# The first two pairs of each MLP with eight block products, and the feature sums made between them

## The chip, the cores and the metric

One core of a Trainium2 chip runs the whole program. The metric is the device time in microseconds, from the start of the program to its end; the median of three runs is compared. TensorE (PE in the rows) multiplies, VectorE (DVE), ScalarE (ACT) and GpSimd (POOL) do the element-wise work, and SyncE (SP) issues the transfers.

## The reference, cut to what matters

Two layers of a backbone over 1280 tokens (1024 latent tokens and a context of 256) with 1024 features; each layer is a mixer and then an MLP with 4096 hidden features and squared ReLU.

```python
def modulate(x, g, shift, scale):
    return (rms_norm(x, g) * (1.0 + scale) + shift).astype(x.dtype)

def sq_relu_mlp(h, w1, w2):
    return jnp.square(jax.nn.relu(h @ w1)) @ w2
...
        yp = yp + (mp[5] * sq_relu_mlp(modulate(yp, norm2_g[l], mp[3], mp[4]), ff_w1[l], ff_w2[l])).astype(yp.dtype)
        ys = ys + (ms[5] * sq_relu_mlp(modulate(ys, norm2_g[l], ms[3], ms[4]), ff_w1[l], ff_w2[l])).astype(ys.dtype)
```

Everything is float32. The kernel splits each operand into a high part (type fp32r) and the low part that is left (`hi`, `lo`), and makes a product of two float32 blocks from three matmuls (hi by hi, hi by lo, lo by hi): this is `three`.

## The kernel before

Activations lie with features on partitions: `hhi[ti]`, `hlo[ti]` are the normalised input of the MLP, [128, 8 feature chunks, tokens], for the token parts ti = 0 (tokens 0 to 511), 1 (512 to 1023) and 2 (the 256 context tokens). They are made by `apply` of a norm object for each token part, which takes the rows of 1/rms that TensorE spreads over the partitions (`rows`: two matmuls, `spread_rows`, L368 and L369, from a diagonal matrix `ndg` that VectorE and ScalarE make, L361 and L362; its input `nrs` comes from a power on GpSimd, L403, and `nst` from VectorE, L401).

`ff1` makes the hidden features in 16 pairs of chunks (128 features each). For the 1024 latent tokens a pair is a 2 by 2 block product: two chunks by two halves of the input features (feature chunks 0 to 3 and 4 to 7) times these halves by two halves of the tokens. Plainly that is eight block products of 12 matmuls (4 feature chunks, `three` for each). The kernel takes seven, as Winograd's variant of Strassen's scheme does: sums of weight blocks (`sum_` on GpSimd, L601, split again by `parts`, L607 and L608, into `s12` and `s34`) times sums of feature blocks (`com[2]`, `com[3]`, `com[4]`, the tiles tb2, tb3 and tb4h/tb4l). The feature sums are made once for an MLP, inside `apply` of token part 1 (tb2 and tb3, through the tiles nd) and of token part 2 (`last_block`: tb4h, tb4l from nd4). The context tokens add 2 times 24 matmuls 256 wide to each pair (`prompt`).

The raw weights of a pair are loaded into four `wraw` slots or, for odd pairs, into one tile with the tag `tt`, which holds nd4 before, and the first feature blocks of `ff2` after. At the end of a pair four differences of hidden blocks are made (L668) and all is written to device memory (`Dt`, `Dh`); `ff2` reads it back (`br`), with its weights in `ar`.

The instructions of each engine stand in one order, which a list scheduler makes at build time; an engine does not go past an instruction that waits. SyncE issues every transfer from one queue. `pend` in `ff1` holds the statistics and the `apply` of token part 2, which are emitted between the first products of pair 0 (`late`).

Of the kernel before, what the change touches and what calls it, by code (L numbers as in the profile page):

```python
# [431 lines left out]
class NormBlocks(Norm):  # L432
# [17 lines left out]
    def apply(self, At, Bt, hhi, hlo):  # L450
        if self.ti == 2:
            Norm.apply(self, At, Bt, hhi, hlo)
            self.last_block()
# [11 lines left out]
        d2, d3 = [[g.fp.tile([128, 2, 512], F32, tag="hid", name="nd", bufs=4) for i in range(2)] for _ in range(2)]
        com["d4"] = g.fp.tile([128, 4, 512], F32, tag="tt", name="nd4", bufs=1)
        x0 = com["x0"]
        for k in range(4):
            u, v = self.scaled(k, pb, At), self.scaled(4 + k, pb, At)
            t, e2, e3 = x0[:, k, :], d2[k // 2][:, k % 2], d3[k // 2][:, k % 2]  # L470
            nc.vector.tensor_tensor(t, u, t, op=ALU.subtract)
            nc.vector.tensor_tensor(e2, v, t, op=ALU.subtract)
            nc.gpsimd.tensor_tensor(e3, v, u, op=ALU.subtract)
            nc.gpsimd.tensor_tensor(com["d4"][:, k], x0[:, 4 + k, :], e2, op=ALU.subtract)
            self.plain(hi[:, k, :], lo[:, k, :], t)
            self.biased(hi[:, 4 + k, :], lo[:, 4 + k, :], v, Bt[:, 4 + k, 0:1])
        for n, (d, tag) in enumerate(((d2, "x0"), (d3, "x1"))):
            t = g.xm.tile([128, 2, 4, 512], F32R, tag=tag, name=f"tb{2 + n}", bufs=1)
            for k in range(4):
                self.biased(t[:, 0, k], t[:, 1, k], d[k // 2][:, k % 2], Bt[:, 4 + k, 0:1] if n == 0 else dsh[:, k:k + 1])  # L480
            com[2 + n] = (t[:, 0], t[:, 1])

    def last_block(self):
        g, com = self.g, self.com
# [81 lines left out]

def ff1(g, l, h, com, pend, Dh, Dt):
# [42 lines left out]

    for p in range(NFC // 2):
# [10 lines left out]
        sum_(a22, a21, a22, ALU.add)  # L622
        sum_(a21, a11, a21)
        sum_(a11, a22, a11)
        sum_(a12, a12, a11)
        s12, s34 = parts((a22, a11), nc.vector), parts((a21, a12), nc.gpsimd)
# [14 lines left out]
        ca = bank(g, "mm")
        product(ca, w1, 0, part(0, 0), True)
        late()
        t = saved(ca)
        ps = bank(g, "w")
        product(ps, w1, 1, part(0, 4), True)
        late()
        add_square(b11, t, ps)
        if p:
# [1 line left out]
        product(ca, s12, 1, com[2], False)
        u1 = saved(ca)
        cb = bank(g, "w")
        product(cb, s12, 0, part(1, 0), True)
        product(ca, s34, 0, com[3], False)
        u2 = saved(ca)
# [3 lines left out]
        prompt(1, w2)  # L660
        product(ca, w2, 1, com[4], False)
        square(b21, ca)
        product(cb, s34, 1, part(1, 4), False)
        add_square(b12, u1, cb)
        ts = []
        for j, (x, y) in enumerate(((b12, b11), (b22, 0), (b22, b12), (b21, 1))):
            ts.append(scratch())
            nc.vector.tensor_tensor(ts[j], x, ts[y] if j % 2 else y, op=ALU.subtract)  # L668
            nc.sync.dma_start(Dt[p, :, j], ts[j])
# [1499 lines left out]
```

## Time and profile before

| | us |
|---|---|
| median of 3 runs | 3257.35 (3252.08 to 3261.74) |
| the profiled execution, its own time | 3254.04 |
| its span, first to last instruction | 3251.1 |
| TensorE busy in the span | 3009.4 (93%) |
| VectorE / ScalarE / GpSimd busy | 2171.6 / 1292.5 / 1286.6 |
| mean granted TensorE clock | 0.965 of full speed |

The two MLPs' first halves (`ff1`) run from about 1067 us to 1530 us and from about 2384 us to 2845 us of the span. A row of a timeline gives the start, the duration, the engine, the line and what is written from what; in brackets stands how long the engine sat idle before it and what it waited for.

### The profile page before, as it was taken

The page shows a single profiled execution, that of the slowest core. Times are in us where ns is not written, and L with a number is a line of the kernel's source. Part 1 is how long each engine was busy: PE and PEld are TensorE (multiplying, and loading weights), DVE is VectorE, ACT ScalarE, POOL GpSimd, SP SyncE. Part 2 cuts the span into 40 slices and gives each one's busy share as a digit, 9 for nine tenths or more (in the row PEclk, how much of TensorE's full clock was granted, in tenths as well). Part 3 has the DMA queues.
Part 4 walks back from the last instruction along what each step waited for, and adds up shares of the span by engine and source line. Part 5 has one row for each costly group of instructions (what it writes and reads, how often), then busy time and mean ns, then how long its engine had stood idle before and what let it go on. Part 6 is the DMA issues. An engine that isn't in the chain of part 4 may idle for free.

```text
span 3251.1 us, 50543 instructions
## 1 busy us (share of the span) xinstructions
PE 3009.4 (93%) x19543; PEld 2411.1 (74%) x19543; DVE 2171.6 (67%) x3278; ACT 1292.5 (40%) x2116; POOL 1286.6 (40%) x861
## 2 busy tenths in 40 slices
PE   8989976899999699999999998998969999999999
PEld 5777754665557588887888877887757888788888
DVE  5548887667742855556877766878276555687776
ACT  5455433453322422222333336778242222333332
POOL 0000004455421645445767631000155444667664
PEclk9999986999999899999999999999989999999999
DMA  5356677546862233336624220110413333464332
GB/s 203 85 142 175 174 181 195 155 125 208 264 226 72 71 111 133 132 133 213 231 92 156 91 98 27 40 39 23 153 38 123 139 127 127 168 238 156 123 111 85
DMA packets 309967, 437.52 MB, mean 135 GB/s; under 512 B 80346, under 2 KB 154874, under 8 KB 309726
## 3 DMA queue, kind: packets, MB, share of 16 engines
q1 hardware_dynamic: 309726, 434.29, 41.8%
q8 instruction: 153, 2.51, 0.3%
q14 instruction: 88, 0.72, 0.1%
HBM read 301.29 MB, written 132.90 MB: 134 GB/s over the span
## 4 chain that ended last, share of the span: by engine, by line
PE 62%; DVE 16%; issue 7%; DMA 4%; ACT 2%; POOL 2%; SPq 1%; DVEq 0%; ACTq 0%; POOLq 0%
PE ps_w L556 7%; PE ps_w L557 7%; PE ps_w L558 7%; PE ps_mm L558 6%; PE ps_mm L556 6%; PE ps_mm L557 6%; PE ps_mm L528 4%; PE ps_mm L529 4%; PE ps_mm L530 4%; DVE ffr L668 2%; DVE prod L1765 2%; PE ps_ad L300 2%; DVE NI L1732 1%; DVE Vinv L1766 1%; DMA ar<-ff 1%
## 5 line engine op out<-in xcount | busy, mean ns | idle before, releaser
L528 PE MATMUL ps_mm<-hhi,whi 128*128 128x512 f32 (+2 forms) x1232 | 447.3, 364 | 19.1 <-ACT hhi L842 13.4
L529 PE MATMUL ps_mm<-hlo,whi 128*128 128x512 f32 (+2 forms) x1232 | 444.9, 362 | 5.2 <-POOL hlo L429 5.2
L530 PE MATMUL ps_mm<-hhi,wlo 128*128 128x512 f32 (+2 forms) x1232 | 444.3, 362 | 1.4 <-POOL wlo L519 1.4
L692 POOL TENSOR_TENSOR wlo<-ar,whi 128x1024 fp32r<-128x1024 f32 x96 | 246.7, 2585 | 269.7 <-ACT whi L691 259.0
L556 PE MATMUL ps_w<-hhi,whi 128*128 128x256 f32 (+1 forms) x896 | 297.9, 333 | 3.2 <-ACT whi L607 3.2
L557 PE MATMUL ps_w<-hlo,whi 128*128 128x256 f32 (+1 forms) x896 | 296.6, 333 | 0.0
L558 PE MATMUL ps_w<-hhi,wlo 128*128 128x256 f32 (+1 forms) x896 | 293.3, 333 | 0.0
L528 PEld LDWEIGHTS ps_mm<-hhi,whi 128*128 128x128 f32 (+1 forms) x1232 | 232.8, 189 | 66.8 <-ACT hhi L842 13.8
L529 PEld LDWEIGHTS ps_mm<-hlo,whi 128*128 128x128 f32 (+1 forms) x1232 | 232.6, 189 | 47.4 <-POOL hlo L429 6.5
L530 PEld LDWEIGHTS ps_mm<-hhi,wlo 128*128 128x128 f32 (+1 forms) x1232 | 233.0, 189 | 43.5 <-issue 5.8
L684 DVE SCALAR_TENSOR_TENSOR x<-ps_mm,mod,x 128x512 f32<-128x512 f32 x272 | 200.7, 746 | 82.2 <-PE ps_mm L558 82.2
L684 DVE SCALAR_TENSOR_TENSOR x<-ps_w,mod,x 128x512 f32<-128x512 f32 (+1 forms) x304 | 185.2, 632 | 96.1 <-PE ps_w L558 95.9
L597 DVE TENSOR_TENSOR hid<-ffr,ps_w 128x512 f32<-128x512 f32 x96 | 65.6, 683 | 244.0 <-ACT ffr L588 230.7
L691 ACT CAST whi<-ar 128x1024 fp32r<-128x1024 f32 x96 | 97.8, 1048 | 277.3 <-PE ps_w L557 207.6
L556 PEld LDWEIGHTS ps_w<-hhi,whi 128*128 128x128 f32 x896 | 170.8, 191 | 24.8 <-ACT whi L607 4.0
L557 PEld LDWEIGHTS ps_w<-hlo,whi 128*128 128x128 f32 x896 | 170.3, 190 | 22.5
L588 ACT COPY ffr<-ps_mm 128x512 f32<-128x512 f32 x96 | 56.4, 587 | 324.0 <-PE ps_mm L558 243.6
L558 PEld LDWEIGHTS ps_w<-hhi,wlo 128*128 128x128 f32 x896 | 169.0, 190 | 18.5
L993 POOL MEMSET pad<- 128x2 f32 (+2 forms) x60 | 3.8, 120 | 443.9 <-DVE xc L1011 203.6
L608 POOL TENSOR_TENSOR wlo<-wraw,whi 128x512 fp32r<-128x512 f32 x64 | 96.5, 1519 | 156.6 <-ACT whi L607 156.6
L608 POOL TENSOR_TENSOR wlo<-raw,whi 128x512 fp32r<-128x512 f32 x64 | 91.6, 1442 | 155.2 <-ACT whi L607 153.9
L556 PE MATMUL ps_w<-pp,whi 128*128 128x256 f32 x512 | 142.9, 282 | 0.6 <-DVE x L684 0.6
(466 smaller groups left out, 8211.6 us busy)
## 6 DMA issues: line engine op xcount, KB each, us to landing
adaw<-ada SPq DMA_DIRECT2D x80, 512.0 KB
dh<-hid SPq DMA_DIRECT2D x64, 512.0 KB
dt<-ffr SPq DMA_DIRECT2D x128, 256.0 KB
br<-dh SPq DMA_DIRECT2D x128, 256.0 KB
ar<-ff SPq DMA_DIRECT2D x128, 256.0 KB
br<-dt SPq DMA_DIRECT2D x128, 256.0 KB
wraw<-w_in SPq DMA_DIRECT2D x76, 256.0 KB
wraw<-ff SPq DMA_DIRECT2D x64, 256.0 KB
```

Of the source, the lines that this page charges most:

```text
L300: nc.tensor.matmul(ps[32 * j:32 * j + 32, :], g.sc[:, k, :], w[:, i, :], start=k == 0, stop=k == KC - 1, skip_group_check=True)
L528: nc.tensor.matmul(ps, whi[:, k, :], hhi[:, k, :], start=first and k == k0, stop=False)
L529: nc.tensor.matmul(ps, whi[:, k, :], hlo[:, k, :], start=False, stop=False)
L530: nc.tensor.matmul(ps, wlo[:, k, :], hhi[:, k, :], start=False, stop=last and k == k1 - 1)
L556: g.nc.tensor.matmul(ps, ah, bh, start=first, stop=False, skip_group_check=True)
L557: g.nc.tensor.matmul(ps, ah, bl, start=False, stop=False, skip_group_check=True)
L558: g.nc.tensor.matmul(ps, al, bh, start=False, stop=last, skip_group_check=True)
L597: nc.vector.tensor_tensor(out, t, ps, op=ALU.add)
L608: e.tensor_tensor(lo[:, c], s, hi[:, c], op=ALU.subtract)
L684: nc.vector.scalar_tensor_tensor(xt[ti][:, o, :], ps[:, :tw], Gt[:, o, cc:cc + 1], xt[ti][:, o, :], op0=ALU.mult, op1=ALU.add)
L691: nc.scalar.copy(hi[:, c], s)
L692: nc.gpsimd.tensor_tensor(lo[:, c], s, hi[:, c], op=ALU.subtract)
```

## The change

- In the first two pairs of each MLP (`NPLAIN = 2`) no weight sums are made, and the eight plain block products are taken (`plain`); the other 14 pairs keep the seven (`seven`).
- `apply` of token part 1 makes only its own high and low parts: of the difference of the two token halves in feature chunks 0 to 3 (which stands there in both kernels), and of the features 4 to 7. The sums com[2] to com[4] are made by a generator, `sums`, which `late` advances between the products of pairs 0 and 1; what is left of it is made at the end of pair 1.
- In the sums, GpSimd's subtractions (L448, L473, L474) go to VectorE. nd2 and nd3 lie in the `tt` tile one after the other; so the loads of raw weights into `tt` are now those of even pairs from pair 2.
- The differences and writes at a pair's end (`finish`) are given a lower priority by 60.

```diff
     def plain(self, hi, lo, t):
         self.g.nc.scalar.copy(hi, t)
-        self.g.nc.gpsimd.tensor_tensor(lo, t, hi, op=ALU.subtract)
+        self.g.nc.vector.tensor_tensor(lo, t, hi, op=ALU.subtract)
...
+        x0 = com["x0"]
+        for k in range(4):
+            u, t = self.scaled(k, pb, At), x0[:, k, :]
+            nc.vector.tensor_tensor(t, u, t, op=ALU.subtract)
+            self.plain(hi[:, k, :], lo[:, k, :], t)
+        for k in range(4, KC):
+            self.biased(hi[:, k, :], lo[:, k, :], self.scaled(k, pb, At), Bt[:, k, 0:1])
+        com["sums"] = self.sums(Bt)
+
+    def sums(self, Bt):
+        g, nc, com = self.g, self.g.nc, self.com
+        x0, x1 = com["x0"], self.x
...
+        d = g.fp.tile([128, 4, 512], F32, tag="tt", name="nd2", bufs=1)
         hi = g.xm.tile([128, 4, 512], F32R, tag="x2", name="tb4h", bufs=1)
         lo = g.fp.tile([128, 4, 512], F32R, tag="t4", name="tb4l", bufs=1)
+        com[4] = (hi, lo)
         for k in range(4):
-            self.plain(hi[:, k], lo[:, k], com["d4"][:, k])
-        com[4] = (hi, lo)
+            nc.vector.tensor_tensor(d[:, k], x1[:, 4 + k, :], x0[:, k, :], op=ALU.subtract)
+            nc.vector.tensor_tensor(x0[:, 4 + k, :], x0[:, 4 + k, :], d[:, k], op=ALU.subtract)
+            self.plain(hi[:, k], lo[:, k], x0[:, 4 + k, :])
+            if k % 2:
+                yield
+        for n, tag in ((2, "x0"), (3, "x1")):
+            if n == 3:
+                d = g.fp.tile([128, 4, 512], F32, tag="tt", name="nd3", bufs=1)
+                for k in range(4):
+                    nc.vector.tensor_tensor(d[:, k], x1[:, 4 + k, :], x1[:, k, :], op=ALU.subtract)
+            t = g.xm.tile([128, 2, 4, 512], F32R, tag=tag, name=f"tb{n}", bufs=1)
+            com[n] = (t[:, 0], t[:, 1])
+            for k in range(4):
+                self.biased(t[:, 0, k], t[:, 1, k], d[:, k], Bt[:, 4 + k, 0:1] if n == 2 else dsh[:, k:k + 1])
+                if k % 2:
+                    yield
...
+NPLAIN, LATER = 2, 60
...
-        if p % 2:
+        if p >= NPLAIN and p % 2 == 0:
             t = pool.tile([128, 2, 2, 512], F32, tag="tt", name="raw", bufs=1)
...
+        def plain():
+            ss = []
+            for i, w in enumerate((w1, w2)):
+                ps = bank(g, "mm")
+                product(ps, w, 0, part(0, 0), True)
+                ss.append(saved(ps))
+                product(ps, w, 1, part(0, 4), False)
+                square(hid[i][:, 0:512], ps)
+                if p:
+                    late()
+            late()
+            for i, w in enumerate((w1, w2)):
+                ps = bank(g, "mm")
+                product(ps, w, 0, part(1, 0), True)
+                product(ps, w, 1, part(1, 4), False)
+                add_square(hid[i][:, 512:1024], ss[i], ps)
+                late()
             prompt(0, w1)
+            prompt(1, w2)
+            late()
...
+        (plain if p < NPLAIN else seven)()
+        if p == NPLAIN - 1:
+            list(com["sums"])
+        with prio(g.tc, -LATER):
+            finish(p, hid, hp)
```

How the order of instructions moves is shown at three places. The first is TensorE in layer 0, from the spread of token part 1's rows (ndg_11066) to that of token part 2's (128x256). hhi0 and hhi1 are the inputs of token parts 0 and 1; the weights 11213 and 11219 (11250 and 11266 before: w1 and s12) are those of pair 0, 11498 and 11504 those of pair 1. Before:

```order
L558 MATMUL ps_w_11313<-hhi0_10927,wlo_11251 128x512
L369 MATMUL ps_w_11139<-ndg_11066,onesr_66 128x512
L347 MATMUL ps_w_10507<-con_60,nt0_11295 128x64
L368 MATMUL ps_w_11326<-ndg_11302,onesr_66 128x256
L369 MATMUL ps_w_11326<-ndg_11302,onesr_66 128x256
L556 MATMUL ps_w_11390<-hhi1_10928,whi_11266 128x512
```

Now, where left-out rows are marked:

```order
L369 MATMUL ps_w_11139<-ndg_11066,onesr_66 128x512
L563 MATMUL ps_mm_11229<-hhi0_10927,whi_11213 128x512
...
L563 MATMUL ps_mm_11305<-hhi1_10928,whi_11213 128x512
L563 MATMUL ps_mm_11370<-hhi1_10928,whi_11219 128x512
L563 MATMUL ps_mm_11514<-hhi0_10927,whi_11498 128x512
...
L347 MATMUL ps_w_10507<-con_60,nt0_11289 128x64
L564 MATMUL ps_mm_11305<-hlo1_10931,whi_11213 128x512
...
L565 MATMUL ps_mm_11370<-hhi1_10928,wlo_11220 128x512
L368 MATMUL ps_w_11332<-ndg_11296,onesr_66 128x256
```

Between the two spreads stood one small transpose; now 96 matmuls of products stand there as well: 24 of pair 0 on token part 0, then 2 of pair 0 that need hhi1, 24 of pair 1 on token part 0, the transpose, and the 46 that are left of pair 0 on token part 1.

The second is VectorE at the same place, from the scaling of token part 1 (L439) to the diagonal of token part 2 (L361); hlo1 is the low part of token part 1. Before:

```order
L439 SCALAR_TENSOR_TENSOR x1_10264<-x1_10264,A02_10247,ps_w_11139 128x512 x8
L401 TENSOR_SCALAR nst_11298<-ps_w_10507 128x2
L471 TENSOR_TENSOR x0_10255<-x1_10264,x0_10255 128x512 x2
L444 SCALAR_TENSOR_TENSOR hlo1_10931<-x1_10264,mod0_71,hhi1_10928 128x512
...
L357 CAST nrh_11303<-nrs_11300 128x2
L472 TENSOR_TENSOR nd_11144<-x1_10264,x0_10255 128x512
L472 TENSOR_TENSOR nd_11145<-x1_10264,x0_10255 128x512 x2
L358 TENSOR_TENSOR nrl_11304<-nrs_11300,nrh_11303 128x2
L444 SCALAR_TENSOR_TENSOR tb3_11198<-nd_11146,dsh_11142,tb3_11198 128x512 x2
L444 SCALAR_TENSOR_TENSOR tb3_11198<-nd_11147,dsh_11142,tb3_11198 128x512
L361 TENSOR_SCALAR ndg_11302<-con_60,nrh_11303 128x128 x2
```

Now:

```order
L439 SCALAR_TENSOR_TENSOR x1_10264<-x1_10264,A02_10247,ps_w_11139 128x512 x8
L465 TENSOR_TENSOR x0_10255<-x1_10264,x0_10255 128x512 x4
L605 TENSOR_TENSOR hid_11225<-ffr_11256 128x512
L444 SCALAR_TENSOR_TENSOR hlo1_10931<-x1_10264,mod0_71,hhi1_10928 128x512 x3
L481 TENSOR_TENSOR nd2_11399<-x1_10264,x0_10255 128x512
...
L448 TENSOR_TENSOR hlo1_10931<-x0_10255,hhi1_10928 128x512 x2
L482 TENSOR_TENSOR x0_10255<-x0_10255,nd2_11399 128x512 x2
L401 TENSOR_SCALAR nst_11292<-ps_w_10507 128x2
L482 TENSOR_TENSOR x0_10255<-x0_10255,nd2_11399 128x512 x2
L357 CAST nrh_11297<-nrs_11294 128x2
L358 TENSOR_TENSOR nrl_11298<-nrs_11294,nrh_11297 128x2
L361 TENSOR_SCALAR ndg_11296<-con_60,nrh_11297 128x128 x2
```

And GpSimd now, from the low part of pair 1's w1 (wlo_11499) over the powers for token parts 1 and 2 (L403) to part 2's low parts (hlo2):

```order
L619 TENSOR_TENSOR wlo_11499<-wraw_11490,whi_11498 128x512
L619 TENSOR_TENSOR wlo_11499<-wraw_11491,whi_11498 128x512
L403 TENSOR_TENSOR nrs_11064<-nst_11062,neghalf_64 128x4
L403 TENSOR_TENSOR nrs_11294<-nst_11292,neghalf_64 128x2
L429 TENSOR_TENSOR hlo2_10932<-nt0_11335,hhi2_10929 128x256
```

Between the two powers GpSimd has nothing now; before, four instructions on pair 0's weight sums stood there, and after the second power 12 instructions of 128x512 for the sums. The low parts of tb3 are gone from here and stand later; four subtractions into hlo1 (L448) and four into x0 (L482) have come from GpSimd, and two squarings of pair 0 stand between. In all 30 instructions of 128x512 stand ahead of L361 on VectorE; 23 did before.

The third is TensorE at the end of layer 0's `ff1`, from pair 14's last product (ps_w_14393 before, ps_w_14382 now) to pair 15's first use of a feature sum (tb2); bb is the first feature block of `ff2`. Before:

```order
L558 MATMUL ps_w_14393<-hhi1_10928,wlo_14312 128x512
L556 MATMUL ps_w_14604<-hhi1_10928,whi_14516 128x512
L557 MATMUL ps_w_14604<-hlo1_10931,whi_14516 128x512
L556 MATMUL ps_w_14633<-hhi2_10929,whi_14506 128x256
...
L556 MATMUL ps_mm_14532<-tb2_11189,whi_14516 128x512
```

Now:

```order
L565 MATMUL ps_w_14382<-hhi1_10928,wlo_14301 128x512
L563 MATMUL ps_mm_14704<-bb_14716,whi_14710 128x512
...
L565 MATMUL ps_mm_14706<-bb_14716,wlo_14711 128x512
L563 MATMUL ps_w_14596<-hhi1_10928,whi_14508 128x512
...
L563 MATMUL ps_mm_14524<-tb2_11544,whi_14508 128x512
```

18 matmuls of `ff2` have come ahead of pair 15's products with weight sums. In layer 1 the three places look the same.

## Rows read from the trace of the kernel before

**Rows 1.** The page's row of each engine's busy time.

```profile
PE 3009.4 (93%) x19543; PEld 2411.1 (74%) x19543; DVE 2171.6 (67%) x3278; ACT 1292.5 (40%) x2116; POOL 1286.6 (40%) x861
```

**Rows 2.** TensorE's waits over the whole span: us in total, times, longest.

```profile
PE ps_w L368 <- DVE ndg L361: 62.2, 6, 27.9
...
PE ps_mm L558 <- DVE wlo L608: 17.9, 26, 2.5
```

**Rows 3.** Stretches of layer 0: length, busy us, clock, share of transfers.

```profile
core 0: us, PE busy (x) PEld busy (x) DVE busy (x) ACT busy (x) POOL busy (x), PEclk, DMA share, GB/s
1067.39:1075.40 8.01, 6.88 (x33) 4.91 (x31) 5.01 (x8) 3.69 (x10) 5.01 (x4) 1.00 0.53 167
1075.40:1103.50 28.10, 0.23 (x2) 0.10 (x1) 28.03 (x29) 8.54 (x14) 21.50 (x13) 0.59 0.03 9
1103.50:1107.60 4.10, 4.04 (x11) 3.29 (x12) 4.07 (x9) 2.30 (x6) 0.91 (x1) 0.50 0.01 2
...
1138.80:1142.00 3.20, 3.20 (x8) 2.57 (x9) 3.00 (x3) 0.00 (x0) 2.75 (x2) 0.53 0.63 193
```

**Rows 4.** The same stretches of layer 1.

```profile
2391.80:2419.90 28.10, 0.23 (x2) 0.09 (x1) 28.04 (x29) 8.54 (x14) 21.50 (x13) 0.55 0.03 9
...
2454.60:2458.00 3.40, 3.37 (x11) 2.67 (x12) 3.06 (x3) 0.00 (x0) 2.80 (x2) 0.70 0.62 189
```

**Rows 5.** TensorE in layer 0, in order of time.

```profile
1068.20 0.40 PE L556 MATMUL ps_mm<-hhi,whi 128*128 128x512 f32 x1
1068.43 0.40 PE L557 MATMUL ps_mm<-hlo,whi 128*128 128x512 f32 x1
...
1071.93 0.47 PE L368 MATMUL ps_w<-ndg,onesr 128*128 128x512 f32 x1 [1.13 <-DVE ndg L361]
...
1103.56 0.55 PE L368 MATMUL ps_w<-ndg,onesr 128*128 128x256 f32 x1 [27.93 <-DVE ndg L361]
```

**Rows 6.** TensorE after that wait, in order of time.

```profile
1104.55 0.63 PE L557 MATMUL ps_w<-hlo,whi 128*128 128x512 f32 x1
1104.98 0.63 PE L558 MATMUL ps_w<-hhi,wlo 128*128 128x512 f32 x1
...
1138.78 0.79 PE L558 MATMUL ps_mm<-tb,wlo 128*128 128x512 f32 x1 [2.47 <-DVE wlo L608]
```

**Rows 7.** VectorE in layer 0, in order of time.

```profile
1075.47 5.36 DVE L439 SCALAR_TENSOR_TENSOR x<-x,A,ps_w 128x512 f32<-128x512 f32 x8 [3.03 <-PE ps_w L369]
...
1080.81 1.28 DVE L471 TENSOR_TENSOR x<-x,x 128x512 f32<-128x512 f32 x2
...
1083.28 1.76 DVE L444 SCALAR_TENSOR_TENSOR hlo<-x,mod,hhi 128x512 fp32r<-128x512 f32 x1
...
1102.94 0.47 DVE L361 TENSOR_SCALAR ndg<-con,nrh 128x128 fp32r<-128x128 f32 x2
```

**Rows 8.** GpSimd in layer 0, in order of time.

```profile
1082.63 3.53 POOL L473 TENSOR_TENSOR nd<-x 128x512 f32<-128x512 f32 x2
...
1096.20 6.27 POOL L474 TENSOR_TENSOR nd<-x,nd 128x512 f32<-128x512 f32 x4
```

**Rows 9.** The chain that ended last, layer 0, in order of time.

```profile
1114.77 5.08 POOL tb4l L448 x4
...
1120.72 4.29 DMA raw<-ff
...
1138.78 0.79 PE ps_mm L558
```

**Rows 10.** One pair of chunks in the middle of layer 0's ff1.

```profile
1253.03:1279.18 26.15, 25.83 (x132) 21.46 (x132) 15.49 (x18) 7.56 (x14) 13.07 (x9) 1.00 0.40 141
```

**Rows 11.** TensorE at the end of layer 0's ff1, in order of time.

```profile
1515.88 0.50 PE L556 MATMUL ps_mm<-tb,whi 128*128 128x512 f32 x1 [3.53 <-ACT whi L607]
1517.01 0.59 PE L558 MATMUL ps_mm<-tb,wlo 128*128 128x512 f32 x1 [0.40 <-DVE wlo L608]
...
1522.64 0.50 PE L556 MATMUL ps_mm<-tb,whi 128*128 128x512 f32 x1 [1.48 <-ACT ffr L588]
```

More of the change, by code (lines that the diff above doesn't have):

```diff
@@ L452, in apply @@
             Norm.apply(self, At, Bt, hhi, hlo)
-            self.last_block()
             return
@@ L463, in apply @@
         dsh = g.cp.tile([128, 4], F32, tag="dsh", name="dsh", bufs=1)
         nc.vector.tensor_tensor(dsh, Bt[:, 4:8, 0], Bt[:, 0:4, 0], op=ALU.subtract)
[L465 to L484, printed above, removed]
+        d = g.fp.tile([128, 4, 512], F32, tag="tt", name="nd2", bufs=1)
         hi = g.xm.tile([128, 4, 512], F32R, tag="x2", name="tb4h", bufs=1)
@@ L609, in parts, with finish @@
         return hi, lo
+    def finish(p, hid, hp):
+        (b11, b12), (b21, b22) = [[t[:, 0:512], t[:, 512:1024]] for t in hid]
+        ts = []
+        for j, (x, y) in enumerate(((b12, b11), (b22, 0), (b22, b12), (b21, 1))):
+            ts.append(scratch())
+            nc.vector.tensor_tensor(ts[j], x, ts[y] if j % 2 else y, op=ALU.subtract)
+            nc.sync.dma_start(Dt[p, :, j], ts[j])
+        for i in range(2):
+            nc.sync.dma_start(Dh[p, :, i, 0:NL], hid[i])
+            nc.sync.dma_start(Dh[p, :, i, NL:], hp[i])
     for p in range(NFC // 2):
-        if p % 2:
+        if p >= NPLAIN and p % 2 == 0:
             t = pool.tile([128, 2, 2, 512], F32, tag="tt", name="raw", bufs=1)
@@ L621, in ff1 @@
         w1, w2 = parts((a11, a12), nc.gpsimd), parts((a21, a22), nc.vector)
[L622 to L626, printed above, removed]
+        if p >= NPLAIN:
+            sum_(a22, a21, a22, ALU.add)
+            sum_(a21, a11, a21)
+            sum_(a11, a22, a11)
+            sum_(a12, a12, a11)
+            s12, s34 = parts((a22, a11), nc.vector), parts((a21, a12), nc.gpsimd)
         hid = [pool.tile([128, 1024], F32, tag="hid", name="hid", bufs=4) for i in range(2)]
@@ L639, in late @@
                 pend.pop(0)()
[L641 to L649, printed above, removed]
-            prompt(0, w1)
[L651 to L656, printed above, removed]
@@ L657, in ff1 @@
-        add_square(b22, u2, cb)
-        if not p:
-            prompt(0, w1)
[L660 to L669, printed above, removed]
@@ L670, in ff1 @@
-        for i in range(2):
-            nc.sync.dma_start(Dh[p, :, i, 0:NL], hid[i])
-            nc.sync.dma_start(Dh[p, :, i, NL:], hp[i])
+            else:
+                next(com["sums"], None)
+        def plain():
[15 more added lines that the diff above has]
+                late()
+            prompt(0, w1)
+            prompt(1, w2)
+            late()
@@ new lines, in seven @@
+        def seven():
+            ca = bank(g, "mm")
+            product(ca, w1, 0, part(0, 0), True)
+            t = saved(ca)
+            ps = bank(g, "w")
+            product(ps, w1, 1, part(0, 4), True)
+            add_square(b11, t, ps)
+            prompt(0, w1)
+            product(ca, s12, 1, com[2], False)
+            u1 = saved(ca)
+            cb = bank(g, "w")
+            product(cb, s12, 0, part(1, 0), True)
+            product(ca, s34, 0, com[3], False)
+            u2 = saved(ca)
+            add_square(b22, u2, cb)
+            prompt(1, w2)
+            product(ca, w2, 1, com[4], False)
+            square(b21, ca)
+            product(cb, s34, 1, part(1, 4), False)
+            add_square(b12, u1, cb)
```

## The prediction

> **What bounds the kernel now.** I read the page's busy times first, then TensorE's waits, then the stretches around the longest of them. TensorE is busy for 93% of the span [rows 1], so time can be won only where it waits or runs at the lower clock. Its longest waits are for the diagonal of token part 2 (L361): 62.2 us in six times, two of them 27.9 us each [rows 2]. These two are where the change works. In layer 0 TensorE spreads part 1's rows and then stands still from 1075.4 to 1103.5 us, while VectorE is busy for all 28.03 us of it [rows 3]; in layer 1 the same stretch has the same 0.23 us of TensorE [rows 4]. The reader should see there that TensorE is not short of work: 15 pairs of products lie behind the spread, held up because its order is fixed, and because VectorE makes the feature sums ahead of the diagonal.
>
> Two things make the stall dearer than its idle time. After it the clock is at 0.50 of full speed (1.2 GHz) for 4.1 us [rows 3], and the wide matmuls follow each other every 0.43 us [rows 6], not every 0.23 [rows 5]. And the sums hold the tile tt until tb4l is done at 1119.85, so pair 1's weights land only at 1125.0, and TensorE waits another 2.47 us at 1138.78 [rows 6, 9], then at 0.53 of the clock for 3.2 us [rows 3]. From there a pair takes 26.15 us, of which TensorE is busy 25.83 [rows 10].
>
> **The change part by part.**
>
> *The gap, layer 0.* Ahead of the change TensorE's waits are 1.13 and 27.93 us [rows 5]. Now 96 wide matmuls stand between the two spreads: 96 x 0.233 = 22.4 us. What could hold them up is VectorE, with 30 instructions of 128x512 ahead of L361. Those of L439 took 5.36/8 = 0.67 us, subtractions 1.28/2 = 0.64; the slow ones (1.76) begin with GpSimd's own 1.77 us subtractions at 1082.6 [rows 7, 8]. In the new order GpSimd has nothing of that size there. So I take 12 x 0.67 + 18 x 0.64 = 19.6 us, and 2.7 for the power and the small instructions (an estimate: 0.47 for L361 [rows 7] and some 2.2 for the rest): 22.3 us. TensorE and VectorE are then done at nearly the same time. Two short waits stay: the first matmul on token part 1 needs all eight scalings, a subtraction and a cast, some 6.6 us, against 24 x 0.233 = 5.6 us of work ahead of it (1.0), and low parts that come one by one (another 1.0). Left: 2.0; won: 29.1 - 2.0 = **27.1 us**. Bounds: 0.5 us left (28.6 won); or VectorE at the mean of the old stretch, 28.03/29 = 0.97 us for each instruction, which makes 29 + 2.7 = 31.7 us and leaves 9.3 idle (19.8 won). I take the first value since the two speeds stand apart in the rows, by whether GpSimd runs.
>
> The Trainium skill ("SBUF — State Buffer", Who interferes with whom) says that VectorE and GpSimd share a pair of ports as an exclusive lock: an instruction of VectorE with two SBUF inputs contends with one of GpSimd that reads SBUF, and the loser blocks. It speaks against putting more on VectorE only where GpSimd still reads. By it the chain is 22 us; by the stretch's mean it would be 31.7, and the kernel some 15 us slower than forecast.
>
> *The clock after the gap.* With waits near 1 us the clock should stay: the 1.13 us wait lies in a stretch at 1.00 [rows 3, 5]. 4.1 us at half speed become 2.1: **2.0 us** won (bounds 0 and 2.0).
>
> *The second stall.* 2.47 idle, and 3.2 us at 0.53 give 1.5: 4.0 us in layer 0; layer 1 has a wait of 2.5 too [rows 2] and 3.4 us at 0.70, 1.0: 3.5 us. What is late next is pair 2: its weights go into tt after tb3. After the second spread TensorE has 72 wide matmuls of pair 1 (16.8 us) and 96 narrow ones (48 of them fill the rest of a pair, (25.83 - 84 x 0.233)/48 = 0.13 each, so 12.5): 29.3 us of cover. VectorE needs about 20 us to the end of tb3 (16 instructions of 0.64 for the sums, and part 2's apply and pair 0's results before or between them, some 9 us by the same rows), then 5.2 us for the load (1119.85 to 1125.0): 25 us, inside the cover. The weight sums took 13.8 us more (1125.0 to 1138.78): 39 us, against 29.3 and another 24 wide and 24 narrow (8.7 us) = 38. I leave 2.0 us of stall: won **2.0 us** in layer 0 and **1.5** in layer 1. Bounds: nothing left (4.0, 3.5); or 8 us of stall (4 lost), if tb3 comes 7 us later.
>
> *The eighth product.* 2 pairs x 12 matmuls x 0.233 = **5.6 us** lost in each layer. Nothing hides it: TensorE is the bound there. Against it stand two pairs without the 0.32 us wait: **0.6** won. The weight sums and s12, s34 that fall away in these pairs were on GpSimd and VectorE beside TensorE: worth nothing by themselves.
>
> *Later results, and tt for even pairs.* Inside ff1 the order of pairs 3 to 14 hardly moves, so no gain there. At its end 18 matmuls of ff2 (4.2 us) come ahead of pair 15's products with weight sums, which wait 3.53 + 0.40 + 1.48 us [rows 11]; they can come because pair 15 no longer holds tt, where ff2's first block goes. I take **3.0 us** for each layer: 4.2 us of cover over 5.4 of waits, less something for part of the waits moving to ff2's loads, which share the transfers with much else. Bounds: all 5.4 and some clock, 7 won; or ff2's block late by a load's 5.2 us beyond, 4 lost.
>
> **Sum.** Layer 0: 27.1 + 2.0 + 2.0 - 5.6 + 0.6 + 3.0 = 29.1; layer 1: 28.6. Together 57.7 us, from the profiled execution's own 3254.0: 3196.3. The median of the runs is 3.3 above that execution, so 3199.6: I predict **3200 us**.
>
> **The rivals.**
> - *The stall moves to pair 2* (17%). Tile tt is free late, because VectorE's sums after the second spread share it with pair 0's results and run at 1.76, not 0.64: 20 instructions x 1.1 = 22 us late, less 4 of slack, 18 a layer at most. For it: GpSimd still makes part 2's low parts and weights there. Against: those are few. Half of the price in each layer gives 3218, the whole 3236.
> - *Pair 1's loads come late* (8%). Its w1 low parts stand on GpSimd ahead of the power that the first spread needs, and its 24 matmuls on TensorE ahead of the 46. The loads (1 MB) share the queue with 1 MB of layer results; at the 167 GB/s of that stretch [rows 3] 2 MB take 12.6 us. If all is exposed, 25 us of the gain go: 3225.
> - *Slower* (6%). VectorE is the new bound between the spreads: if all 30 instructions took 1.76 us, the diagonal would come 55.5 us after the first spread, 27.4 later than now, for 22.4 us of products: with the 5.6 us lost and the other terms some 6 us a layer slower, about 3270. It decides from a mean of about 1.5 us for an instruction. For it: 1.76 is what these same lines cost today in half of the stretch. Against: it is measured beside GpSimd alone.
> - *No change* (4%). TensorE waits for both, the loads and the sums, so that about 26 us a layer come back: within 0.3%, some 10 us, which is about what a measurement of this kernel tells from nothing.
> - *More than forecast* (3%): all stalls gone and the end of ff1 smooth, 28.6 + 2.0 + 4.0 - 5.6 + 0.6 + 7 = 36.6 a layer: 3184 and below.
>
> My own case, 3184 to 3214, has 62%. The range of **3182 to 3230** leaves out the slower case, no change, and the far end of the first two rivals: some 15%. Chances: faster by over 0.3% 0.88 (forecast, more, and the first two rivals, less a little of their far ends), the same 0.06, slower 0.06.
>
> **What would show each step.** In the profile after: the wait of L368 for L361 near 1103 falls from 27.9 us to 3 or less, and TensorE is over 20 us busy between the two spreads, at a clock of 1.00; VectorE's 30 instructions there take 0.6 to 0.7 us each; TensorE waits no more than 3 us at the start of pair 2; and the waits at the end of ff1 are shorter. The count of wide matmuls rises by 48. I am wrong if VectorE's instructions keep 1.7 us without GpSimd, if the load of pair 2's weights begins later than some 21 us after the second spread, or if TensorE waits for bb at the end of ff1.

## The result, and the profile after

The changed kernel takes 3201.38 us (median of four runs, 3192.70 to 3203.33) against 3255.37 (four runs, 3252.08 to 3261.74). The ratio, taken from the mean times and not from the medians, is 0.9827, with an interval of 0.9803 to 0.9851. In a second comparison it took 3198.93 against 3258.57, 0.9814 (0.9798 to 0.9830). Predicted were 3200 us.

The page's busy row of the changed kernel:

```profile
PE 3017.9 (94%) x19591; PEld 2415.0 (75%) x19591; DVE 2138.5 (67%) x3298; ACT 1282.7 (40%) x2100; POOL 1195.4 (37%) x805
```

TensorE has 48 matmuls more, as it should: 2 layers x 2 pairs x 12. Its waits over the whole span (in total, times, longest):

```profile
PE ps_mm L565 <- DVE wlo L619: 13.0, 24, 1.4
PE ps_mm L563 <- ACT ffr L599: 11.6, 8, 3.1
...
PE ps_w L368 <- DVE ndg L361: 3.5, 2, 2.3
...
PE ps_w L564 <- DVE bl L737: 2.7, 1, 2.7
```

The wait for the diagonal is down from 62.2 us to 3.5 [rows 2], and those 3.5 lie behind layer 0's `ff2` (at 1918.8 and 1952.8 us). Windows of the changed kernel: the start of ff1 to the first context product of pair 2, and the stretch between the two spreads, for layer 0 and then layer 1.

```profile
core 0: us, PE busy (x) PEld busy (x) DVE busy (x) ACT busy (x) POOL busy (x), PEclk, DMA share, GB/s
1076.81:1143.59 66.78, 65.56 (x336) 53.93 (x334) 52.61 (x94) 28.81 (x59) 14.16 (x12) 1.00 0.23 80
1083.60:1108.00 24.40, 23.18 (x99) 17.88 (x98) 21.02 (x37) 7.04 (x14) 1.61 (x1) 1.00 0.04 15
2365.60:2432.87 67.27, 65.82 (x337) 53.89 (x334) 52.63 (x92) 28.77 (x59) 13.07 (x12) 1.00 0.22 79
2372.40:2397.00 24.60, 23.38 (x100) 18.08 (x99) 21.01 (x37) 7.04 (x14) 1.62 (x1) 1.00 0.04 18
```

The same start before the change (to the same matmul of pair 2):

```profile
1067.39:1163.63 96.24, 63.40 (x311) 52.12 (x310) 69.68 (x85) 34.33 (x67) 56.04 (x38) 0.84 0.22 77
```

96.24 us have become 66.78. In the one TensorE was busy for 63.40 us at a mean clock of 0.84, in the other for 65.56 at 1.00 (2.4 GHz). Between the spreads it is busy for 23.18 of 24.40 us, where it had 0.23 of 28.10 [rows 3]. TensorE in order of time shows what is left of the 27.93 us [rows 5]:

```profile
1082.95 0.50 PE L368 MATMUL ps_w<-ndg,onesr 128*128 128x512 f32 x1
...
1087.71 0.50 PE L563 MATMUL ps_mm<-hhi,whi 128*128 128x512 f32 x1 [1.22 <-ACT ffr L599]
...
1107.98 0.28 PE L368 MATMUL ps_w<-ndg,onesr 128*128 128x256 f32 x1
```

The second spread no longer waits. One wait of 1.22 us stands: pair 0's second bank is copied by ScalarE (L599) before TensorE adds to it. VectorE, beside it:

```profile
1083.72 5.36 DVE L439 SCALAR_TENSOR_TENSOR x<-x,A,ps_w 128x512 f32<-128x512 f32 x8 [4.35 <-PE ps_w L369]
1089.00 2.49 DVE L465 TENSOR_TENSOR x<-x,x 128x512 f32<-128x512 f32 x4
...
1103.51 0.48 DVE L361 TENSOR_SCALAR ndg<-con,nrh 128x128 fp32r<-128x128 f32 x2
...
1127.77 2.07 DVE L444 SCALAR_TENSOR_TENSOR tb<-nd,dsh,tb 128x512 fp32r<-128x512 f32 x3
```

The scalings take 0.67 us each as before [rows 7], the others 0.62 to 0.74; no 1.76 us instruction is left ahead of the diagonal. The last row is the end of tb3, at 1129.84. GpSimd then idles almost throughout (24.37 us ahead of the power), and SyncE asks for pair 2's weights as soon as tb3 is done:

```profile
1101.58 1.61 POOL L403 TENSOR_TENSOR nrs<-nst,neghalf 128x2 f32<-128x2 f32 x1 [24.37 <-DVE nst L401]
```

```profile
1129.87 1.75 SPq L641 DMA_DIRECT2D raw<-ff  x4
```

They come in time: TensorE has no wait from 1100 to 1150 us, where before the second stall stood [rows 6].

Nearly the whole gain, 58.1 of 60.7 us in the profiled executions, lies at the start of ff1. I measure it from the spread of token part 0's rows to the first matmul on tb4h in pair 7, by which time the order is the same in both kernels. Before, layer 0:

```profile
1047.39 0.39 PE L368 MATMUL ps_w<-ndg,onesr 128*128 128x512 f32 x1
...
1316.20 0.40 PE L556 MATMUL ps_mm<-tb4h,whi 128*128 128x512 f32 x1
```

After:

```profile
1056.81 0.39 PE L368 MATMUL ps_w<-ndg,onesr 128*128 128x512 f32 x1
...
1296.21 0.40 PE L563 MATMUL ps_mm<-tb4h,whi 128*128 128x512 f32 x1
```

That is 268.81 and 239.40 us. From pair 7 to pair 13 all kernels then take 156.9 to 157.9 us (6 x 26.15 is 156.9, [rows 10]). The table has this start for every profiled execution below, and the rest: all from that first spread (1047.39 us in the execution before the change) to the end of the span. What lies ahead of it took 1047.4 to 1059.9 us in these executions, though the order there is that of before; the rest leaves this out.

```
run                    median   ratio [interval]          start, layer 0 / 1   rest
before                                                    268.8 / 268.5        2203.7
the change             3201.4   0.9827 [0.9803, 0.9851]   239.4 / 239.8        2143.0
change_again           3198.9   0.9814 [0.9798, 0.9830]   239.7 / 239.5        2143.4
no_plain_pairs         3260.3   0.9995 [0.9984, 1.0006]   267.3 / 267.3        2200.1
no_plain_wraw          3229.9   0.9907 [0.9892, 0.9921]   257.7 / 256.7        2174.5
one_plain              3232.9   0.9907 [0.9886, 0.9927]   253.3 / 254.2        2176.0
one_plain_wraw         3230.5   0.9912 [0.9890, 0.9934]   251.8 / 256.4        2177.1
one_plain_free_first   3228.1   0.9906 [0.9890, 0.9922]   255.0 / 254.3        2175.7
three_plain            3202.6   0.9819 [0.9801, 0.9837]   242.8 / 242.5        2150.2
subs_on_gpsimd         3217.9   0.9863 [0.9840, 0.9885]   248.4 / 252.2        2164.0
tt_odd                 3201.9   0.9822 [0.9809, 0.9836]   241.0 / 240.9        2146.7
later_0                3198.3   0.9810 [0.9797, 0.9824]   239.8 / 239.6        2141.8
last_pair_first        3205.5   0.9836 [0.9821, 0.9851]   239.6 / 239.8        2157.9
```

One of the four executions of subs_on_gpsimd took 10056.67 us at a mean granted clock of 0.433, and its row leaves it out.

### The profile page after: what moved, and what is told of

Same layout as the page of the kernel before. It is cut to its first block, busy times and chain, and to the rows that moved or that the text cites. A ratio compares the mean times of both kernels' runs of the same rounds, so it can differ in the third digit from the quotient of the medians.

```text
span 3199.8 us, 50542 instructions
## 1 busy us (share of the span) xinstructions
PE 3017.9 (94%) x19591; PEld 2415.0 (75%) x19591; DVE 2138.5 (67%) x3298; ACT 1282.7 (40%) x2100; POOL 1195.4 (37%) x805
## 4 chain that ended last, share of the span: by engine, by line
PE 65%; DVE 14%; issue 7%; DMA 4%; ACT 2%; POOL 1%; SPq 1%; DVEq 0%; ACTq 0%; POOLq 0%
PE ps_mm L565 7%; PE ps_w L563 7%; PE ps_w L564 7%; PE ps_w L565 7%; PE ps_mm L563 7%; PE ps_mm L564 7%; PE ps_mm L535 5%; PE ps_mm L536 5%; PE ps_mm L537 5%; DVE ffr L627 2%; DVE prod L1805 2%; PE ps_ad L300 2%; DVE Vinv L1806 1%; PE ps_w L2164 1%; PE ps_w L2160 1%
## 5 line engine op out<-in xcount | busy, mean ns | idle before, releaser
L563 PE MATMUL ps_w<-hhi,whi 128*128 128x512 f32 (+1 forms) x848 | 276.5, 326 | 0.6 <-DVE hid L608 0.3
L564 PE MATMUL ps_w<-hlo,whi 128*128 128x512 f32 (+1 forms) x848 | 275.3, 326 | 0.0
L565 PE MATMUL ps_w<-hhi,wlo 128*128 128x512 f32 (+1 forms) x848 | 272.0, 327 | 0.0
L608 DVE TENSOR_TENSOR hid<-ffr,ps_w 128x512 f32<-128x512 f32 x84 | 57.3, 682 | 213.0 <-ACT ffr L599 201.4
L563 PEld LDWEIGHTS ps_w<-hhi,whi 128*128 128x128 f32 x848 | 159.6, 188 | 20.0 <-ACT whi L618 1.0
L564 PEld LDWEIGHTS ps_w<-hlo,whi 128*128 128x128 f32 x848 | 159.5, 188 | 19.6
L565 PEld LDWEIGHTS ps_w<-hhi,wlo 128*128 128x128 f32 x848 | 158.0, 188 | 15.7
L599 ACT COPY ffr<-ps_mm 128x512 f32<-128x512 f32 x92 | 54.0, 587 | 283.9 <-PE ps_mm L565 214.0
L619 POOL TENSOR_TENSOR wlo<-wraw,whi 128x512 fp32r<-128x512 f32 x64 | 93.6, 1474 | 180.0 <-ACT whi L618 180.0
L619 POOL TENSOR_TENSOR wlo<-raw,whi 128x512 fp32r<-128x512 f32 x56 | 83.0, 1495 | 163.8 <-ACT whi L618 163.8
```

Of the source, the lines that this page charges most:

```text
L563: g.nc.tensor.matmul(ps, ah, bh, start=first, stop=False, skip_group_check=True)
L564: g.nc.tensor.matmul(ps, ah, bl, start=False, stop=False, skip_group_check=True)
L565: g.nc.tensor.matmul(ps, al, bh, start=False, stop=last, skip_group_check=True)
L619: e.tensor_tensor(lo[:, c], s, hi[:, c], op=ALU.subtract)
```

## The experiments

All start from the changed kernel. The theory: products that need no sum cover VectorE's chain between the spreads. The rivals: it is enough that the subtractions left GpSimd; or one pair is enough.

**No eight-product pairs** (`no_plain_pairs`); `seven` gets the `late` calls and pair 0's place of `prompt` back as before the change, and odd pairs use tt again.

```diff
-NPLAIN, LATER = 2, 60
+NPLAIN, LATER = 0, 60
...
+    list(com["sums"])
     for p in range(NFC // 2):
-        if p >= NPLAIN and p % 2 == 0:
+        if p % 2:
...
```

> The changed kernel without its eight-product pairs: all 16 pairs take seven products, the sums are made ahead of pair 0 (on VectorE, as in the change), the results stay late. My theory (the gain is cover: products between the two spreads): some 25 instructions of 0.6 us now stand ahead of the diagonal, so the gap shrinks from 28 to about 19 us and no more, since nothing fills it; some 9 us a layer are won, about 3237 us (3225 to 3246), and TensorE still waits 15 to 20 us for the diagonal in each layer. Rival (the gain is that GpSimd's subtractions left, and the products cost more than they cover): 3210 or less. Rival (only the cover counts, the move to VectorE is worth nothing): 3250 to 3258.

The gap did what the theory said, the time did not: 3260.3 us against 3261.0 before, which is no change. It lies in none of the three forecasts; the nearest is the 3250 to 3258 of the rival by which only cover counts, though the gap did shrink. TensorE's longest waits at the start of layer 0 in this run:

```profile
PE ps_w L368 <- DVE ndg L361: 17.5, 2, 16.4
PE ps_mm L565 <- DVE wlo L619: 3.2, 2, 1.7
PE ps_mm L563 <- ACT tb L443: 2.5, 1, 2.5
PE ps_mm L563 <- ACT whi L618: 1.3, 1, 1.3
```

The wait for the diagonal is 16.4 instead of 27.9, and the spreads stand 20.1 us apart instead of 31.6. But the start as a whole is only 1.5 us shorter: 10 of the 11.5 us came back behind the spread. There pair 0 waits for its own sums (tb), and pair 1's weights, which go into tt, are asked for only after tb3. The clock was 0.91 from 1110 to 1130 us.

```profile
1118.92 1.75 SPq L642 DMA_DIRECT2D raw<-ff  x4
```

**The same, pair 1's weights in wraw** (`no_plain_wraw`), to see which of the two it was; the edit is against the run before.

```diff
-        if p % 2:
+        if p and p % 2 == 0:
             t = pool.tile([128, 2, 2, 512], F32, tag="tt", name="raw", bufs=1)
```

> The run without eight-product pairs once more (its rest was 2200.1, before 2203.7), with tt for even pairs from pair 2, so that pair 1's weights need not wait for the sums to leave tt. My theory (the 11 us a layer won at the gap came back because nothing independent was ready after it: part of that pair 1's weights, asked for only at 1118.9): some 24 wide matmuls of pair 1 fill the time after the second spread, 4 to 7 us a layer: 2186 to 2193. Rival (pair 0's own need for the sums gives it all back, the loads don't matter): 2198 to 2202. Rival (the load in tt was the whole of it): 2178 to 2182.

All three were too small: the starts fell by 9.6 and 10.5 us more. The weights are now asked for ahead of the sums, and TensorE's waits show what that took away:

```profile
1069.20 5.95 SPq L642 DMA_DIRECT2D wraw<-ff  x4
```

```profile
PE ps_w L368 <- DVE ndg L361: 17.6, 2, 16.4
...
PE ps_mm L565 <- DVE wlo L619: 0.6, 1, 0.6
```

The wait for the diagonal is still 16.4 us; those for the cast of tb (2.5) and for pair 1's weights (1.3) are gone, and the clock from 1110 to 1130 us is 1.00 where it was 0.91. So, taken in this order, of the 29.4 us by which layer 0's start has become shorter, the moves alone bring 1.5, a load that does not hang on tt 9.6, and the eight-product pairs 18.3; in layer 1 it is 1.2, 10.5 and 16.9. The rest fell by 25.7 us in all; 2.7 and 4.1 of these came at the ends of the two ff1, where tt now goes to even pairs.

**Subtractions back on GpSimd** (`subs_on_gpsimd`).

```diff
-        self.g.nc.vector.tensor_tensor(lo, t, hi, op=ALU.subtract)
+        self.g.nc.gpsimd.tensor_tensor(lo, t, hi, op=ALU.subtract)
...
-            nc.vector.tensor_tensor(x0[:, 4 + k, :], x0[:, 4 + k, :], d[:, k], op=ALU.subtract)
+            nc.gpsimd.tensor_tensor(x0[:, 4 + k, :], x0[:, 4 + k, :], d[:, k], op=ALU.subtract)
...
-                    nc.vector.tensor_tensor(d[:, k], x1[:, 4 + k, :], x1[:, k, :], op=ALU.subtract)
+                    nc.gpsimd.tensor_tensor(d[:, k], x1[:, 4 + k, :], x1[:, k, :], op=ALU.subtract)
```

> The changed kernel with 16 of the 20 subtractions that left GpSimd put back there (the low parts of plain, the second step of tb4, the differences of nd3); eight-product pairs and order of making kept. My theory: VectorE and GpSimd hold each other up when both read two operands of SBUF, VectorE's 0.6 us become about 1.7 wherever GpSimd works; between the spreads some 8 GpSimd instructions of 1.7 us make 14 us in which VectorE does a third of its rate, so the diagonal comes some 6 us later, TensorE waits 4 to 8 us for it or for low parts, and the tile tt comes free later, 0 to 8 us more in each layer: about 3215 us (3206 to 3232). Rival (the two engines do not disturb each other, GpSimd only takes work off): VectorE's instructions stay at 0.6 us, 3199 to 3204.

The time, 3217.9 us, is in the range. VectorE and GpSimd in layer 0:

```profile
1090.02 5.19 DVE L444 SCALAR_TENSOR_TENSOR hlo<-x,mod,hhi 128x512 fp32r<-128x512 f32 x3
1095.13 1.77 DVE L481 TENSOR_TENSOR nd<-x,x 128x512 f32<-128x512 f32 x1
...
1133.24 2.73 DVE L444 SCALAR_TENSOR_TENSOR tb<-nd,dsh,tb 128x512 fp32r<-128x512 f32 x4
```

```profile
1088.71 7.63 POOL L448 TENSOR_TENSOR hlo<-x,hhi 128x512 fp32r<-128x512 f32 x4 [11.86 <-ACT hhi L447]
...
1116.39 3.80 POOL L448 TENSOR_TENSOR tb4l<-x,tb4h 128x512 fp32r<-128x512 f32 x3
```

L444 takes 5.19/3 = 1.73 us and L481 1.77, both beside GpSimd's L448; the same L444 takes 2.73/4 = 0.68 when GpSimd is still. GpSimd pays too: 7.63/4 = 1.91 us for L448 beside VectorE, 3.80/3 = 1.27 while VectorE idles. Not as I said, the diagonal was hardly later (the spreads stand 25.1 us apart, 25.0 in the change): with 8 of the 30 instructions gone from VectorE ahead of it, the slower ones just fill the cover. The price came at pair 2: tb3 ends 29.9 us after the second spread instead of 21.9, and TensorE waits for the weights:

```profile
1139.33 0.79 PE L563 MATMUL ps_mm<-hhi,whi 128*128 128x512 f32 x1 [4.14 <-ACT whi L618]
```

The Trainium skill ("SBUF — State Buffer", Who interferes with whom) calls the pair of ports that the two engines share an exclusive lock, and has the order of issue decide who blocks. This trace agrees: as an estimate from its own rows, taking turns would make 0.64 + 1.27 = 1.9 us of either, close to the 1.73 to 1.91 measured. Turns are not the rule everywhere: in `one_plain_wraw` below GpSimd alone is held up, and by VectorE instructions that begin after it, which the page's order of issue does not give.

**One eight-product pair** (`one_plain`).

```diff
-NPLAIN, LATER = 2, 60
+NPLAIN, LATER = 1, 60
```

> NPLAIN = 1: only pair 0 takes eight products. 2.8 us a layer are saved; 79 wide matmuls, 18.4 us, are left between the spreads against VectorE's 20.3, a wait of about 2 us; and pair 2's weights, which need the tile tt after tb3 (21.8 us after the second spread in the changed kernel) and 5 us of load, are wanted about 22 us after it: a wait of 4 to 8 us. My theory (both pairs are needed as cover): 3207 to 3219 us, most likely 3211, with the wait at the start of pair 2. Rival (one pair covers the sums, the second is paid for nothing): 3194 to 3198.

Both pairs are needed, by more than I said: the time, 3232.9 us, is beyond my 3207 to 3219, and the starts are 13.9 and 14.4 us longer. TensorE's waits from 1065 to 1300 us:

```profile
PE ps_mm L565 <- DVE wlo L619: 5.3, 6, 2.3
PE ps_mm L563 <- ACT ffr L599: 5.2, 2, 4.0
PE ps_mm L564 <- DVE hlo L448: 2.2, 1, 2.2
```

They make some 15 us with smaller ones, and the clock fell with them (0.91 to 0.93 from 1105 to 1175 us). None of these is the wait for pair 2's own weights that I had forecast. The longest, 4.0 us, is for a copy that ScalarE made after 6.35 us of idling for which the profile shows no cause; 3.4 of the 5.3 are for low parts of weight sums (at 1160.0 and 1192.5 us).

**The same, pair 2's weights in wraw** (`one_plain_wraw`): NPLAIN = 1, and `if p > 1 and p % 2:` decides on tt.

> The run with one eight-product pair once more (its rest was 2176.0; the rest runs from the spread of token part 0's rows in layer 0 to the end), with pair 2's weights in wraw instead of tt, so that they need not wait for the sums; tt from pair 3, odd pairs. My theory (what one pair of cover lacks is mostly the late load of pair 2 behind the sums, as without eight-product pairs, where the same move gave 25.6 us): the waits at the start of pair 2 fall, 10 to 13 us a layer are won: rest 2150 to 2157. Rival (one pair covers too little for the sums themselves; TensorE waits for tb2 and tb3): 2166 to 2176.

My theory fell: the time is that of one_plain, near the rival's. The load is late in wraw too, for another reason. TensorE, then ScalarE, SyncE, GpSimd and VectorE:

```profile
1138.20 0.80 PE L563 MATMUL ps_mm<-hhi,whi 128*128 128x512 f32 x1 [6.42 <-ACT whi L618]
```

```profile
1121.09 2.57 ACT L443 ACTIVATE tb<-nd,mod 128x512 fp32r<-128x512 f32 x4 [1.67 <-DVE tb4l L448]
1123.56 1.12 ACT L618 CAST whi<-wraw 128x512 fp32r<-128x512 f32 x2
...
1137.53 0.62 ACT L618 CAST whi<-wraw 128x512 fp32r<-128x512 f32 x1 [5.19 <-DMA wraw<-ff]
```

```profile
1126.46 6.32 SPq L641 DMA_DIRECT2D wraw<-ff  x2
```

```profile
1125.55 6.87 POOL L619 TENSOR_TENSOR wlo<-wraw,whi 128x512 fp32r<-128x512 f32 x1 [6.24 <-ACT whi L618]
```

```profile
1125.71 1.29 DVE L619 TENSOR_TENSOR wlo<-wraw,whi 128x512 fp32r<-128x512 f32 x2
...
1127.25 2.49 DVE L490 TENSOR_TENSOR nd<-x 128x512 f32<-128x512 f32 x4
```

Pair 2 reuses the slots of pair 1, which takes seven products and holds them until its sums of weights are split. That split (1123.56) stands on ScalarE right behind the cast of tb2 (1121.09); SyncE asks for the first quarter of pair 2's weights at 1126.46, but for the second only at 1132.44, and TensorE waits 6.42 us. The second quarter's slot is held by GpSimd's low part of a weight sum. That instruction took 6.87 us, while VectorE ran its own L619 and the sums' L490 beside it at 0.62 to 0.64 us each, as if alone. The same line on GpSimd takes 1.28 us at 1138.23. At that speed the request would stand 5.6 us earlier (an estimate from these rows), which is most of the wait. Layer 1 has the same 6.87 us, and so has `one_plain` (6.89 and 6.87).

There are four slots for split weights (L985), and the sums of pair 1 need the two that pair 0 uses up to its context products: I take this to be why the split itself stands so late, but no run shows it. An eight-product pair needs two slots and gives its raw weights back right after the first split.

**The products that need no sum first** (`one_plain_free_first`), for the cover at one eighth product less.

```diff
+            if p == NPLAIN:
+                cb = bank(g, "mm")
+                product(cb, s12, 0, part(1, 0), True)
+                nc.scalar.copy(b22, cb)
+                product(cb, s34, 1, part(1, 4), False)
+                nc.scalar.copy(b12, cb)
+                prompt(0, w1)
+                prompt(1, w2)
+                product(ca, s12, 1, com[2], False)
+                add_square(b12, b12, ca)
+                product(ca, s34, 0, com[3], False)
+                add_square(b22, b22, ca)
...
```

> As the run before it, and pair 1 takes its products that need no sum of features first (w1's two, s12 by token part 1, s34 by token part 1, its context products) and the three with sums after them; two copies by ScalarE take the place of saved u1 and u2. My theory: pair 1's own products then cover the sums for the price of one eighth product less in each layer (2.8 us) than the change pays: rest 2138 to 2146, at or a little under the changed kernel's 2143.0. Rival (the order on TensorE lets tb2 be waited for all the same): 2150 to 2160.

A miss, at a rest of 2175.7 us: the longest wait, 8.3 us, is again for the weights of pair 2, and GpSimd's L619 again takes 6.86 us ahead of the load.

**Three eight-product pairs** (`three_plain`): NPLAIN = 3.

> NPLAIN = 3: pair 2 takes eight products too. My theory: no stall is left between the spread and pair 2, so the third pair only costs its 12 matmuls, 12 x 0.233 = 2.8 us a layer less about 0.3: 3206 us (3204 to 3209), no wait removed anywhere. Rival (the seven-product pairs at the start still wait for sums of weights, or the sums still hold something up): 3197 to 3201.

The time, 3202.6 us, lies between my 3204 to 3209 and the rival's 3197 to 3201, so it can't tell; the starts can. They are 3.1 and 3.0 us longer than in change_again, where 12 x 0.233 = 2.8 were to be paid and 0.3 to come back. A third pair only costs.

**Tile tt for odd pairs** (`tt_odd`): `if p >= NPLAIN and p % 2:`.

> The changed kernel with tile tt given to odd pairs again (from pair 3), so pair 2's weights go into wraw slots that are long free, and pair 15 holds tt at the end of ff1 as before the change. Judged by the rest: the time from the spread of token part 0's rows in layer 0 to the end, which leaves out the first 1050 us that differ by up to 9 us between executions (before 2203.7, the change 2143.0). My theory: the start of pair 2 waits for nothing in the changed kernel, so nothing is won there, and the end of ff1, where the other parity was to bring 3 us a layer, brought 1.6 us in both layers together: 2141 to 2147. Rival (the even parity is what helps at the end of ff1): 2148 to 2153. Rival (the tile still delays pair 2): 2136 to 2140.

As expected. The starts are 1.3 us longer, and from pair 13 of layer 0's ff1 to the first spread behind its ff2, where the other parity was to help, it is 465.6 us against 465.7 and 463.1 in two executions of the change; in layer 1, to the end, 459.6 against 457.5 and 461.3.

**No lower priority** (`later_0`): LATER = 0.

> LATER = 0: the differences and writes at a pair's end get no lower priority. The rest as defined for the run before it (the change 2143.0). My theory: in the first two pairs they are emitted after all sums anyhow, so VectorE makes up to 8 of them, 0.6 us each, ahead of some sums, and the rest changes by no more than 3 us: 2140 to 2147. Rival (the low priority keeps the results off VectorE's chain of sums and is worth much): 2150 or more.

As expected; it makes no difference that these runs can tell.

**The last pair first** (`last_pair_first`).

```diff
-        (plain if p < NPLAIN else seven)()
+        with prio(g.tc, 400 if p == NFC // 2 - 1 else 0):
+            (plain if p < NPLAIN else seven)()
```

> The products of pair 15, the last, get a higher priority (by 400), so that ScalarE's two copies that free TensorE's bank stand ahead of ff2's cast of a weight difference, for which ScalarE waited 3.76 us at 1500.2 in the changed kernel. My theory: the waits of 3.06 us for the copy at the end of ff1 go, in both layers; the rest 2136 to 2139 against 2143.0, the time some 5 us lower, ratio to before 0.980 to 0.983. Rival (TensorE then waits for the sums of weights or for ff2's tiles instead): 2142 to 2146.

This was to mend what the changed kernel waits for at the end of ff1, here TensorE in layer 0 and ScalarE beside it:

```profile
1495.11 0.50 PE L563 MATMUL ps_mm<-tb,whi 128*128 128x512 f32 x1 [0.37 <-ACT ffr L599]
...
1501.39 0.50 PE L563 MATMUL ps_mm<-tb,whi 128*128 128x512 f32 x1 [3.06 <-ACT ffr L599]
...
1506.62 0.50 PE L563 MATMUL ps_mm<-tb4h,whi 128*128 128x512 f32 x1 [0.68 <-ACT ffr L599]
...
1516.02 0.67 PE L564 MATMUL ps_w<-bl,whi 128*128 128x512 f32 x1 [2.72 <-DVE bl L737]
```

```profile
1500.23 0.62 ACT L731 CAST whi<-wraw 128x512 fp32r<-128x512 f32 x1 [3.76 <-POOL wraw L812]
1500.76 0.58 ACT L599 COPY ffr<-ps_mm 128x512 f32<-128x512 f32 x1
```

The wait for the copy fell from 3.06 to 0.7 us at most, but TensorE's waits from 1470 to 1560 us then were these:

```profile
PE ps_w L563 <- DVE hid L608: 3.0, 1, 3.0
...
PE ps_mm L563 <- ACT ffr L599: 2.6, 4, 0.7
PE ps_mm L564 <- DVE bb L738: 1.8, 2, 1.5
```

They make 11 us with smaller ones, where it was 7.1: the rival was right in what it said of the waits, though its 2142 to 2146 was too low (2157.9). From pair 13 on it was 2.7 to 9.0 us slower in each layer than the two executions of the change; these two differ by up to 3.8 us there themselves, and the profiled execution was one of the two longest of five. No version here is faster than the change by more than the runs can tell.

**The change again** (`change_again`).

> The changed kernel itself once more, as a measure of how far executions differ: the rest within 3 us of 2143.0, the time ahead of it anywhere from 1047 to 1057 us, the ratio to before 0.980 to 0.985.

The rest is within 0.5 us, what lies ahead of it was 4 us shorter (1052.8). In the change the starts agree within 0.4 us over two layers and two executions, so differences of 1 us can be read from one execution; of the whole time they can't. Kernels that stall there scatter more: the two layers of one_plain_wraw differ by 4.6 us.

## Why the prediction was right, and where it was off

The gain at the start of ff1 was put at 26.1 us for layer 0 (27.1 + 2.0 + 2.0 - 5.6 + 0.6) and 25.6 for layer 1, and measured at 29.4 and 28.7. The end of ff1 was put at 3.0 each, and brought 0.8 on the mean. The errors nearly cancel: 57.7 predicted, 60.7 measured in the rest, of which what lay ahead took 9.4 back in the execution that was compared. That 3201.4 lies so near to 3200 is partly luck: what lies ahead varies by 12 us, and the two comparisons gave 54.0 and 59.6 us between the medians.

- **The gap.** Right. Of the wait of 27.9 us the moves took 11.5 and cover the other 16.4: without the eight-product pairs the wait is 16.4 us, with them nothing at the second spread. VectorE's chain was put at 22.3 us and took 20.3 (1083.72 to 1103.99); 1.2 us of waits were left, not 2.0, and not the two that I named (for token part 1's scalings and low parts) but one for a copy.
- **VectorE beside GpSimd.** Right: 0.62 to 0.74 us alone. The choice of this speed over the mean of 0.97 was the step on which the forecast stood; subs_on_gpsimd shows the slow speed. In the rival of a slower kernel, the 55.5 us count from VectorE's first scaling and not, as it says, from the first spread; it did not come true.
- **The clock.** Right: over the start of layer 0 TensorE's busy time grew by 2.2 us (63.40 to 65.56), while 24 wide matmuls more are 5.6. So the clock gave back 3.4 us, where 2.0 behind the gap and 1.5 behind the second stall were put.
- **The second stall.** This is the larger part of what the start gave beyond the forecast: 2.0 us were to stay, none did. tb3 came 21.9 us after the second spread, put at 20. One of my signs of being wrong, a load of pair 2 that begins later than some 21 us after the spread, thus came about and nothing waited: the first cast of these weights began at 1132.80, 2.9 us after the request where I put 5.2, and their first matmul stood at 1138.34, after 30.4 us of cover where I put 29.3. That a later tb3 does cost, subs_on_gpsimd showed: 8.0 us later, 9.0 us more in layer 0.
- **The eighth product.** Right: the third pair cost 3.0 us where 2.5 were worked out.
- **The end of ff1.** Put too high. From pair 13 to the spread behind ff2 (layer 0) or the end (layer 1), the change was 2.0 slower and 4.2 faster in one execution, 0.6 and 0.4 faster in the other: 0.8 us on the mean of four, not 3.0. The stretch scatters by up to 5.9 us among the executions with tt for even pairs, so four values tell little. Over all the executions but last_pair_first it took 464.0 and 458.3 us on the mean with tt for even pairs (seven executions, layer 0 and 1), and 465.3 and 460.5 with tt for odd pairs (five): the gain is there, and a little over half of what I put. The 18 matmuls of ff2 do cover pair 15's sums of weights (the matmul that waited 3.53 us [rows 11] waits 0.37 now), but 3.06 us then go to a copy that stands behind a cast of ff2 on ScalarE, and 2.72 to bl, the low part of another feature block of ff2; my sign was a wait for bb.
- **What the prediction did not see.** It took the two pairs for cover alone. no_plain_wraw shows that with seven products in every pair 10 us of each start hung on the load into tt. With one eight-product pair TensorE waits in part for pair 2's weight sums (one_plain, 3.4 us with pair 3's) or for its weights (one_plain_wraw, 6.42 us). In the second case pair 1's weight sums hold the slots, and one low part of them takes GpSimd 6.87 us beside VectorE's feature sums. The rival of a stall that moves to pair 2 did not come true in the change; something like it is what one pair less gives. The rival of no change is what the moves alone give.

## What to carry to other kernels

A chain that is shortened ahead of one wait gives the time back at the next if nothing independent is ready there: 11.5 us won at the diagonal became 1.5. Count the cover in us against the chain, and with it the slots: a plainer product that takes more matmuls may pay because it needs fewer operands and frees its buffers sooner. When a transfer is asked for late, look at what holds its buffer: here it was one GpSimd instruction of 6.87 us. Measure a local change over a local stretch between two instructions that both kernels have; there 1 us could be told, in the whole time not 5.
